# Second product of an MLP, in blocks of two row tiles by two column groups, every second block with seven products of block sums instead of eight

## The chip, the cores and the metric

One core of a Trainium2 chip runs the kernel. The metric is device time in microseconds (us) of the whole program, a median over runs. The profile comes from one execution, whose engines are PE (TensorE, matrix products; PEld is its loading of stationary operands), DVE (VectorE), ACT (ScalarE), POOL (GpSimd) and SP (SyncE, which issues the DMAs).

## The reference

One encoder layer on 256 tokens of width 2048: attention in two groups of heads, cross-attention to 256 memory tokens, then the part that is changed, with `x` of 256 x 2048, `w_mlp_in` of 2048 x 8192 and `w_mlp_out` of 8192 x 2048:

```
def squared_relu_mlp(h, w_mlp_in, w_mlp_out):
    return jnp.square(jax.nn.relu(h @ w_mlp_in)) @ w_mlp_out

        ff = squared_relu_mlp(x, w_mlp_in[l], w_mlp_out[l])
        x = layer_norm(ALPHA * x + ff, ln3_g[l], ln3_b[l])
```

All data is float32.

## The kernel before

Precision. Each float32 operand is written as a high and a low part: `split` lets ACT round the source to the high part (line 79) and DVE subtract it from the source to give the low part (line 80). A product is three matmuls, high by high, high by low and low by high (`mm3`, lines 145 to 147). Weights come from HBM in units of 1 MB, 128 x 2048, into one of three `raw` buffers; half a unit at a time, 128 x 1024, is split into `w_hi` and `w_lo`, of which there are four buffers each (`wsp`). I call such a split piece a part. So ACT and DVE can be four parts ahead of PE, and a part's buffer comes free when PE has used it for the last time.

The MLP. The 8192 hidden columns are worked off in four chunks (`c`, 16 row tiles of 128 each). In a chunk the first product makes the 16 tiles of the hidden activation in four groups of four (`hidden_group`, its matmuls are lines 194 and 199); `hidden` squares each one and splits it into `ht` (128 hidden rows, then 256 tokens high and 256 low). Then the second product goes over four column groups of 512 (`n`); for each one, `proj_tokens` and `tokens_mm` go over the 16 row tiles `k` and the two blocks `b` of 128 tokens, with a piece of `ht` stationary and 512 weight columns moving. The two sums, one for each token block, stand in PSUM and are added to `res` by DVE (line 755 or 758) when all 16 tiles are in. PSUM has eight tiles of 128 x 512 in two sets of four, `acc` and `att`, and successive groups alternate between the sets, so a group never waits for the tiles of the one before it. In the last chunk the fourth column group is done token block by token block, from parts that were all split ahead (`last_weights`, buffers `w0` and `w1`), so that the layer norm of block 0 runs under the products of block 1.

The order of the instructions on each engine is set when the program is built, by a scheduler that plays a timeline of its own. An engine takes its instructions in that order, and each waits for its semaphores. GpSimd has no work in the MLP but two small powers at the end.

Of the kernel before, what the change touches and what calls it, by code (L numbers as in the profile page):

```python
# [11 lines left out]
F32 = mybir.dt.float32  # L12
F32R = mybir.dt.float32r
# [5 lines left out]
P = 128  # L19
# [19 lines left out]
def encoder_kernel(ctx: ExitStack, tc: tile.TileContext, t, out):  # L39
# [6 lines left out]
    midp = ctx.enter_context(tc.tile_pool(name="midp", bufs=1))  # L46
    resp = ctx.enter_context(tc.tile_pool(name="resp", bufs=2))
    tmp = ctx.enter_context(tc.tile_pool(name="tmp", bufs=7))
    ptp = ctx.enter_context(tc.tile_pool(name="ptp", bufs=2))
    small = ctx.enter_context(tc.tile_pool(name="small", bufs=6))  # L50
    psA = ctx.enter_context(tc.tile_pool(name="psA", bufs=4, space=bass.MemoryType.PSUM))
    psT = ctx.enter_context(tc.tile_pool(name="psT", bufs=4, space=bass.MemoryType.PSUM))

# [23 lines left out]
    def split(hi, lo, src, scale=None, pinned=False):  # L77
        if scale is None:
            pin(nc.scalar.activation(hi, src, AF.Copy), pinned)  # L79
            return pin(nc.vector.tensor_tensor(out=lo, in0=src, in1=f(hi), op=ALU.subtract), pinned)  # L80
# [413 lines left out]
    def stats_tile():  # L494
        return [small.tile([P, 5, 6], F32, tag="bn", name="bn"), 0]
# [204 lines left out]
            w_mi0.append(s_mi0.next())  # L700


    s_in, s_mo = Stream(t["w_mi"][4:]), Stream(t["w_mo"])
    sts = [stats_tile() for _ in range(NB)]

    def hidden(ps, ht, j):
        tt = tmp_tile()
        lo, h = tt[:, 0:S], tt[:, S:2 * S]
        nc.scalar.activation(lo, ps[:, S:2 * S], AF.Copy)
        nc.vector.tensor_tensor(out=h, in0=ps[:, 0:S], in1=lo, op=ALU.add)  # L710
        nc.vector.scalar_tensor_tensor(out=lo, in0=h, scalar=0.0, in1=h, op0=ALU.max, op1=ALU.mult)
        split(ht[:, j, 0:S], ht[:, j, S:2 * S], lo)

    def last_weights(k):

        hi, lo = wide_w[0][:, k * 512:(k + 2) * 512], wide_w[1][:, k * 512:(k + 2) * 512]
        u, h = divmod(k, 4)
        if h == 0:
            wide_w[2] = raw_tile()
            nc.sync.dma_start(wide_w[2], t["w_mo"][s_mo.ap.shape[0] - 4 + u])  # L720
        split(hi, lo, wide_w[2][:, h * 512:(h + 2) * 512])
        return hi, lo

    G = 4

    def hidden_group(nexts, tiles, ht, j0):
# [7 lines left out]
        for i in range(G):  # L734
            hidden(outs[i], ht, j0 + i)

    for c in range(NCH):
        ht = big3(f"ht{c}")
        for g in range(CH // G):
            first = c == 0 and g == 0  # L740
            hidden_group((lambda k: w_mi0[k // 2]) if first else (lambda k: s_in.next()),
                         att_tile if g % 2 else acc_tile, ht, g * G)
            if first:
                side.extend(residual("ln2"))
        for n in range(4):
            tiles = att_tile if n >= 2 else acc_tile
            if c == NCH - 1 and n == 3:
                wide_w = [big.tile([P, 8192], F32R, tag="big", name=f"w{i}") for i in range(2)] + [None]
                ps = proj_tokens(None, ht, CH, 512, by_block=True, wide=last_weights, tiles=tiles)
            else:  # L750
                ps = proj_tokens(s_mo, ht, CH, 512, by_block=False, tiles=tiles)
            for b, o, w, p_ in ps:
                r = res[b][:, n * 512 + o:n * 512 + o + w]
                if c == 0:
                    nc.vector.scalar_tensor_tensor(out=r, in0=r, scalar=ALPHA, in1=p_[:, :w],
                                                   op0=ALU.mult, op1=ALU.add)
                else:
                    nc.vector.tensor_tensor(out=r, in0=r, in1=p_[:, :w], op=ALU.add)
                if c == NCH - 1:
                    stats(sts[b], r)  # L760

    g3, b3 = raw_tile(), raw_tile()
# [44 lines left out]
def _layout(i):  # L807
    f32 = np.float32
    a = {}
    x = np.asarray(i["x"])[0]  # L810
    a["x"] = x
    a["xT"] = np.ascontiguousarray(x.T.reshape(4, 4, P, S).transpose(0, 2, 1, 3)).reshape(4, P, 4 * S)
    a["mem"] = np.asarray(i["mem"])[0]
    w = np.asarray(i["w_in"])[0]
    qa, ka, va, cq, ckv, kr = np.split(w, np.cumsum([1024, 256, 256, 512, 512]), axis=1)
    a["w_qa"] = _rows(_pairs(qa, DH), 4, 512)
    a["w_ka"] = _rows(_pairs(ka, DH), 8, 256)
    a["w_vkr"] = _rows(np.concatenate([va, _pairs(kr, ROPE)], axis=1), 4, 320)
# [34 lines left out]
    a["w_mo"] = np.concatenate([_rows(mo[c * CH * P:(c + 1) * CH * P], 4, 512) for c in range(NCH)])  # L853
# [42 lines left out]
```

## Time and profile before

| what | us |
|---|---|
| median of three runs (lowest, highest) | 1122.93 (1122.74, 1123.06) |
| the profiled execution, time | 1123.25 |
| the same, span of the trace | 1121.4 |
| PE busy in the span | 1105.5 |
| DVE, ACT, POOL busy in the span | 729.0, 537.0, 38.2 |
| first product, chunk 0 (402.29 to 492.80 of the span) | 90.51 |
| first product, chunks 1 and 2 | 89.76 each |
| second product, chunks 0, 1 and 2 | 87.04 each |
| second product, chunk 3 | 87.85 |

The MLP is 710 us of the span. A stage's length here is the time from its first matmul to the first one of the next stage, on PE. The trace's time for one instruction includes a start and an end that overlap its neighbours', so what an instruction costs in a row of many is read from the distance of their starts.

### The profile page before, as it was taken

To read this page: it belongs to the slowest core of one execution; us is meant where nothing else is said; L and a number is where in the kernel's file an instruction comes from. 1 tells how busy PE (TensorE), PEld (TensorE's weight loads), DVE (VectorE), ACT (ScalarE), POOL (GpSimd) and SP (SyncE) were. 2 spreads that over 40 slices of the span, in tenths; PEclk is the share of its full clock that TensorE was granted. 3 is DMA by queue.
4 is the path that set the end of the run, shared out by engine and by line. 5 is a ranking of instruction groups with operands and counts; after the bars stand their busy time and mean duration, and the time that the engine had idled before them with its cause. 6 is when DMAs were issued, how large, how long until landed. Compare 5 with 4: busy or idle time off the path is not lost.

```text
span 1121.4 us, 15079 instructions
## 1 busy us (share of the span) xinstructions
PE 1105.5 (99%) x6004; PEld 954.2 (85%) x6004; DVE 729.0 (65%) x1036; ACT 537.0 (48%) x778; POOL 38.2 (3%) x45
## 2 busy tenths in 40 slices
PE   9999999999999989999999999999999999999996
PEld 6988899888998878888888888888888888888885
DVE  5878677687788677854545565555556454665575
ACT  6555565546576344543344454334444333544440
POOL 1402000000100000000000000000000000000000
PEclk9999999999999999999999999999999999999999
DMA  9664454476467426655555555555555555555562
GB/s 336 224 225 151 150 188 150 151 240 239 162 224 262 150 75 225 204 205 193 188 189 189 188 186 192 195 198 177 208 188 188 193 188 188 188 188 188 191 259 76
DMA packets 37942, 215.85 MB, mean 192 GB/s; under 512 B 4336, under 2 KB 5232, under 8 KB 14192
## 3 DMA queue, kind: packets, MB, share of 16 engines
q1 hardware_dynamic: 37872, 214.89, 54.6%
q8 instruction: 47, 0.77, 0.3%
q14 instruction: 23, 0.19, 0.1%
HBM read 212.78 MB, written 2.10 MB: 192 GB/s over the span
## 4 chain that ended last, share of the span: by engine, by line
PE 96%; DMA 2%; DVE 1%; ACT 0%; issue 0%; SPq 0%; POOL 0%; DVEq 0%; ACTq 0%
PE acc L146 12%; PE acc L145 12%; PE acc L147 12%; PE acc L194 11%; PE att L194 11%; PE att L147 6%; PE att L145 6%; PE att L146 6%; PE acc L199 5%; PE att L199 5%; PE acc L187 2%; PE acc L185 2%; PE acc L186 2%; PE att L534 1%; PE att L349 1%; DMA raw<-in_w_ka 1%
## 5 line engine op out<-in xcount | busy, mean ns | idle before, releaser
L80 DVE TENSOR_TENSOR w_lo<-raw,w_hi 128x1024 fp32r<-128x1024 f32 (+2 forms) x374 | 444.6, 1193 | 327.4 <-ACT w_hi L79 326.3
L79 ACT ACTIVATE w_hi<-raw 128x1024 fp32r<-128x1024 f32 (+2 forms) x374 | 386.5, 1036 | 459.0 <-PE acc L147 171.0
L194 PE MATMUL att<-x2t,w_hi 128*128 128x512 f32 x512 | 139.6, 394 | 0.0
L194 PE MATMUL acc<-x2t,w_hi 128*128 128x512 f32 x480 | 130.9, 394 | 0.0
L145 PE MATMUL acc<-w_hi,ht 128*128 128x512 f32 x256 | 99.6, 389 | 0.0
L146 PE MATMUL acc<-w_lo,ht 128*128 128x512 f32 x256 | 99.6, 389 | 0.0
L147 PE MATMUL acc<-w_hi,ht 128*128 128x512 f32 x256 | 99.6, 389 | 0.0
L194 PEld LDWEIGHTS att<-x2t,w_hi 128*128 128x128 f32 x512 | 88.1, 189 | 12.3
L194 PEld LDWEIGHTS acc<-x2t,w_hi 128*128 128x128 f32 x480 | 82.5, 189 | 11.5
L146 PE MATMUL att<-w_lo,ht 128*128 128x512 f32 x224 | 87.1, 389 | 0.0
L147 PE MATMUL att<-w_hi,ht 128*128 128x512 f32 x224 | 87.1, 389 | 0.0
L145 PE MATMUL att<-w_hi,ht 128*128 128x512 f32 x224 | 87.0, 389 | 0.0
L199 PEld LDWEIGHTS att<-x2t,w_lo 128*128 128x128 f32 x512 | 77.5, 189 | 10.2
L199 PEld LDWEIGHTS acc<-x2t,w_lo 128*128 128x128 f32 x480 | 72.6, 189 | 9.5
L199 PE MATMUL att<-x2t,w_lo 128*128 128x256 f32 x512 | 80.2, 281 | 0.0
L199 PE MATMUL acc<-x2t,w_lo 128*128 128x256 f32 x480 | 75.1, 281 | 0.0
L146 PE MATMUL acc<-w_lo,xt 128*128 128x512 f32 (+2 forms) x192 | 69.5, 363 | 0.2 <-DVE w_lo L80 0.2
L147 PE MATMUL acc<-w_hi,xt 128*128 128x512 f32 (+2 forms) x192 | 69.1, 361 | 0.0
L145 PE MATMUL acc<-w_hi,xt 128*128 128x512 f32 (+2 forms) x192 | 66.1, 364 | 1.0 <-ACT w_hi L79 1.0
L147 PEld LDWEIGHTS acc<-w_hi,ht 128*128 128x128 f32 x256 | 48.0, 188 | 10.0
L145 PEld LDWEIGHTS acc<-w_hi,ht 128*128 128x128 f32 x256 | 48.0, 188 | 10.0
L146 PEld LDWEIGHTS acc<-w_lo,ht 128*128 128x128 f32 x256 | 48.0, 188 | 10.0
(221 smaller groups left out, 1738.1 us busy)
## 6 DMA issues: line engine op xcount, KB each, us to landing
raw<-in_w_mi SPq DMA_DIRECT2D x64, 1024.0 KB, 4.8
raw<-in_w_mo SPq DMA_DIRECT2D x64, 1024.0 KB, 4.8
raw<-in_w_out SPq DMA_DIRECT2D x16, 1024.0 KB, 4.9
raw<-in_w_b SPq DMA_DIRECT2D x5, 1024.0 KB, 4.8
raw<-in_w_qa SPq DMA_DIRECT2D x16, 256.0 KB, 5.4
raw<-in_w_qa SPq DMA_DIRECT2D x4, 1024.0 KB, 4.9
raw<-in_w_ckv SPq DMA_DIRECT2D x4, 1024.0 KB, 5.1
raw<-in_w_cq SPq DMA_DIRECT2D x4, 1024.0 KB, 4.8
```

Of the source, the lines that this page charges most:

```text
L79: pin(nc.scalar.activation(hi, src, AF.Copy), pinned)
L80: return pin(nc.vector.tensor_tensor(out=lo, in0=src, in1=f(hi), op=ALU.subtract), pinned)
L145: nc.tensor.matmul(ps, ah, bh, start=start, stop=False)
L146: nc.tensor.matmul(ps, ah, bl, start=False, stop=False)
L147: nc.tensor.matmul(ps, al, bh, start=False, stop=stop)
L185: nc.tensor.matmul(ps, hi, xt[:, k, 0:S], start=k == 0, stop=False)
L186: nc.tensor.matmul(ps, hi, xt[:, k, S:2 * S], start=False, stop=False)
L187: nc.tensor.matmul(ps, lo, xt[:, k, 0:S], start=False, stop=k == nk - 1)
L194: nc.tensor.matmul(ps, hi[:, i * P:(i + 1) * P], xt[:, k, :], start=k == 0, stop=k == nk - 1)
L199: nc.tensor.matmul(ps[:, 0:S], lo[:, i * P:(i + 1) * P], xt[:, k, 0:S], start=False, stop=False)
L349: nc.tensor.transpose(pp[:, st * S + b * P:st * S + b * P + P], ev[:, b, st * P:(st + 1) * P], ident)
L534: nc.tensor.transpose(ps[:, o:o + P], x(b, k // 4)[:, (k % 4 + j) * P:(k % 4 + j + 1) * P], ident)
```

## The change

The second product takes two row tiles (k, k+1) and two column groups (1024 columns) at a time; I call this a unit. A unit is a 2 x 2 block product: A is two token blocks by two row tiles, B is two row tiles by two column groups, which makes eight block products of three matmuls each. Units go in a chunk by `q` (which half of the 2048 columns) and `p` (which pair of row tiles, 0 to 7). An even `p` is done with its eight block products (24 matmuls) in two parts. An odd `p` is done with seven (21 matmuls), by a scheme of Strassen's kind with sums of blocks: the sums of A are made on DVE in `hidden` and kept in `sums_h`; the sums of B are made on GpSimd, four additions of 128 x 512 for each odd unit, in `load_unit`; and these sums are split as weights are. Such a unit has four parts, of 1024, 512, 1024 and 1024 columns; I call them S1 (two blocks of B), S2 (one block), S3 and S4 (the sums). An even unit's two parts are E1 and E2. The last half of the last chunk (`c` 3, `q` 1) stays as it was. That leaves seven halves with four odd units each, 28 in all.

For a half, `pair_product` holds all eight PSUM tiles: `x11` to `x22` in `acc`, and the products `p1`, `p5`, `p6`, `p7` in `att`. When its units are done, `p1` is copied by ACT, and twelve additions bring the eight tiles into `res`: eight read PSUM and run on DVE; the last four read only SBUF and run on DVE for `q` 0, on GpSimd for `q` 1. The next half, or the next chunk's first product, needs the same eight tiles.

Buffers: `ht` is one tile for all chunks, `wx` is a new one that holds two units' `raw2` and two units' `sums_w`, and the pools of the attention are closed to make room for `sums_h`. `w_mo` is laid out in the new order.

```
@@ hidden @@
-        split(ht[:, j, 0:S], ht[:, j, S:2 * S], lo)
+        return lo
+    def hidden(ps, j):
+        r = []
+        for i in range(2):
+            r.append(square(ps[i]))
+            split(ht[:, j + i, 0:S], ht[:, j + i, S:2 * S], r[i])
+        if strassen(j // 2):
+            (a11, a21), (a12, a22) = [(x[:, 0:P], x[:, P:S]) for x in r]
+            s = tmp_tile()
+            s1, s2, s3, s4 = [s[:, o:o + P] for o in range(0, 4 * P, P)]
+            for o, a, b, op in ((s1, a21, a22, ALU.subtract), (s3, a11, a21, ALU.subtract),
+                                (s2, s1, a11, ALU.subtract), (s4, a12, s2, ALU.add)):
+                nc.vector.tensor_tensor(out=o, in0=a, in1=b, op=op)
+            split(sums_h[:, j // 4, 0, :], sums_h[:, j // 4, 1, :], s)
+    def strassen(p):
+        return p % 2 == 1
@@ new functions @@
+    def load_unit(chunk):
+        if not units or units[0][0] != chunk:
+            return
+        c, q, p = units.pop(0)
+        seven = strassen(p)
+        raw = raw_tile() if seven else raw2[p // 2 % 2]
+        nc.sync.dma_start(raw, t["w_mo"][(c * 2 + q) * (CH // 2) + p])
+        s = None
+        if seven:
+            s = sums_w[p // 2 % 2]
+            b12, b22, b21 = [raw[:, o:o + 512] for o in (0, 1024, 1536)]
+            def add(out, a, b):
+                nc.gpsimd.tensor_tensor(out=out, in0=a, in1=b, op=ALU.add)
+            add(s[:, 0:512], raw[:, 512:1024], b12)
+            add(s[:, 1024:1536], s[:, 0:512], b22)
+            add(s[:, 512:1024], b22, b12)
+            add(s[:, 1536:2048], s[:, 1024:1536], b21)
+        loaded.append((raw, s))
+    def pair_product(c, q):
+        x11, x12, x21, x22 = [acc_tile() for _ in range(4)]
+        p1, p5, p6, p7 = [att_tile() for _ in range(4)]
+        n = CH // 2
+        for p in range(n):
+            load_unit(c)
+            raw, s = loaded.popleft()
+            k = 2 * p
...
+            if strassen(p):
+                first, last = p == 1, p == n - 1
+                for src, todo in ((raw[:, 512:1536], ((p1, a(k, 0), first), (x12, sm(3), False))),
+                                  (raw[:, 1536:2048], ((x11, a(k + 1, 0), False),)),
+                                  (s[:, 0:1024], ((p5, sm(0), first), (p7, sm(2), first))),
+                                  (s[:, 1024:2048], ((p6, sm(1), first), (x21, a(k + 1, 1), False)))):
+                    for (hi, lo), (ps, (ah, al), start) in zip(part(src), todo):
+                        mm3(ps, ah, al, hi, lo, start, last)
+            else:
+                for i in range(2):
+                    w = part(raw[:, i * 1024:(i + 1) * 1024])
+                    for (hi, lo), to in zip(w, ((x12, x22), (x11, x21))):
+                        for b in range(2):
+                            ah, al = a(k + i, b)
+                            mm3(to[b], ah, al, hi, lo, p == 0 and i == 0, to[b] is x22 and p == n - 2 and i == 1)
...
+        rest = nc.gpsimd if q == 1 else nc.vector
+        first_add(r22, x22)
+        m1 = tmp_tile()
+        nc.scalar.activation(m1, p1, AF.Copy)
+        first_add(r12, x12)
+        first_add(r11, x11)
+        add(r12, r12, p5)
+        add(r22, r22, p5)
...
+        add(u2, m1, p6)
+        add(u3, u2, p7)
+        first_add(r21, x21)
+        add(r11, r11, m1, eng=rest)
+        add(r12, r12, u2, ALU.subtract, rest)
+        add(r21, r21, u3, eng=rest)
+        add(r22, r22, u3, ALU.subtract, rest)
...
@@ the loop over chunks @@
+            if g == CH // G - 1:
+                load_unit(c)
+                load_unit(c)
...
+        for q in range(2):
+            if c < NCH - 1 or q == 0:
+                pair_product(c, q)
+                continue
```

GpSimd, which has nothing to do in the MLP before, gets 112 additions for the weights' sums, in the order of the units, and behind each chunk's last unit four for `res`.

PE within the second product of chunk 0, before: for one row tile, the two token blocks (`att_5430`, `att_5431`) in turn, three matmuls each.

```order
L147 MATMUL att_5431<-w_hi_5502,ht0_4233 128x512
L145 MATMUL att_5430<-w_hi_5502,ht0_4233 128x512
L146 MATMUL att_5430<-w_lo_5503,ht0_4233 128x512
L147 MATMUL att_5430<-w_hi_5502,ht0_4233 128x512
L145 MATMUL att_5431<-w_hi_5502,ht0_4233 128x512
L146 MATMUL att_5431<-w_lo_5503,ht0_4233 128x512
```

And now, within half `q` 0 of chunk 0: the end of an odd unit (part S4 is `w_hi_5278` and `w_lo_5279`) and the start of the even unit behind it (E1 is `w_hi_5289` and `w_lo_5290`).

```order
L146 MATMUL att_5058<-w_hi_5278,sums_h_4239 128x512
L146 MATMUL acc_5054<-w_hi_5278,ht_4238 128x512
L146 MATMUL acc_5053<-w_hi_5289,ht_4238 128x512
L147 MATMUL att_5058<-w_lo_5279,sums_h_4239 128x512
L148 MATMUL att_5058<-w_hi_5278,sums_h_4239 128x512
L147 MATMUL acc_5054<-w_lo_5279,ht_4238 128x512
L148 MATMUL acc_5054<-w_hi_5278,ht_4238 128x512
L146 MATMUL acc_5055<-w_hi_5289,ht_4238 128x512
L146 MATMUL acc_5052<-w_hi_5289,ht_4238 128x512
L146 MATMUL acc_5054<-w_hi_5289,ht_4238 128x512
L147 MATMUL acc_5053<-w_lo_5290,ht_4238 128x512
L148 MATMUL acc_5053<-w_hi_5289,ht_4238 128x512
```

The scheduler has put the products with high parts ahead of those that need the low ones. E1 stands in the buffers that S1 of the odd unit had; S1's last matmul is nine ahead of the first row here, so that E1's low part is first needed 19 matmuls after it.

DVE in chunk 1, before, where one column group ends and the next one is under way (the splits on both sides belong to the next groups):

```order
L80 TENSOR_TENSOR w_lo_6674<-raw_6671,w_hi_6673 128x1024
L758 TENSOR_TENSOR res0_1487<-res0_1487,acc_6495 128x512
L758 TENSOR_TENSOR res1_1488<-res1_1488,acc_6496 128x512
L80 TENSOR_TENSOR w_lo_6690<-raw_6671,w_hi_6689 128x1024
L80 TENSOR_TENSOR w_lo_6708<-raw_6705,w_hi_6707 128x1024
```

And now, where half `q` 0 of chunk 1 ends: from part S4 of its last unit (`w_lo_6823`) to S2 of the second unit of `q` 1 (`w_lo_6906`), with E1 and E2 of the first one (`w_lo_6858`, `w_lo_6874`) between; `acc_6522` is `x21`.

```order
L81 TENSOR_TENSOR w_lo_6823<-wx_4240,w_hi_6822 128x1024
L843 TENSOR_TENSOR res0_1487<-res0_1487,acc_6521 128x512
L843 TENSOR_TENSOR res0_1487<-res0_1487,acc_6520 128x512
L81 TENSOR_TENSOR w_lo_6858<-wx_4240,w_hi_6857 128x1024
L846 TENSOR_TENSOR res0_1487<-res0_1487,att_6525 128x512
L846 TENSOR_TENSOR res1_1488<-res1_1488,att_6525 128x512
L81 TENSOR_TENSOR w_lo_6874<-wx_4240,w_hi_6873 128x1024
L846 TENSOR_TENSOR res0_1487<-res0_1487,tmp_6833 128x512
L846 TENSOR_TENSOR tmp_6840<-tmp_6833,att_6526 128x512
L843 TENSOR_TENSOR res1_1488<-res1_1488,acc_6522 128x512
L81 TENSOR_TENSOR w_lo_6896<-raw_6789,w_hi_6895 128x1024
L81 TENSOR_TENSOR w_lo_6906<-raw_6789,w_hi_6905 128x512
```

Two additions between splits have become twelve, woven into the splits of the next half.

PE where the second product of chunk 0 ends and the first product of chunk 1 begins, before: the last matmul of the one, then the four tiles of the first group in turn.

```order
L147 MATMUL att_5431<-w_hi_5552,ht0_4233 128x512
L194 MATMUL acc_5571<-x2t_4110,w_hi_5577 128x512
L194 MATMUL acc_5572<-x2t_4110,w_hi_5577 128x512
L194 MATMUL acc_5573<-x2t_4110,w_hi_5577 128x512
L194 MATMUL acc_5574<-x2t_4110,w_hi_5577 128x512
L199 MATMUL acc_5571<-x2t_4110,w_lo_5578 128x256
```

And now (`acc_5382` is `x21`, and `acc_5704` takes its place in PSUM):

```order
L148 MATMUL acc_5382<-w_hi_5675,ht_4238 128x512
L195 MATMUL acc_5701<-x2t_4110,w_hi_5707 128x512
L195 MATMUL acc_5702<-x2t_4110,w_hi_5707 128x512
L195 MATMUL acc_5703<-x2t_4110,w_hi_5707 128x512
L200 MATMUL acc_5701<-x2t_4110,w_lo_5708 128x256
L200 MATMUL acc_5702<-x2t_4110,w_lo_5708 128x256
```

Further on in the same group, on PE, the fourth tile comes in for the first time:

```order
L195 MATMUL acc_5701<-x2t_4110,w_hi_5749 128x512
L195 MATMUL acc_5702<-x2t_4110,w_hi_5749 128x512
L195 MATMUL acc_5703<-x2t_4110,w_hi_5749 128x512
L195 MATMUL acc_5704<-x2t_4110,w_hi_5707 128x512
L200 MATMUL acc_5704<-x2t_4110,w_lo_5708 128x256
```

The fourth tile's first matmul has moved behind 15 matmuls of 512 columns and 12 of 256.

More of the change, by code (lines that the diff above doesn't have):

```diff
@@ L45, in encoder_kernel @@
     wsp = ctx.enter_context(tc.tile_pool(name="wsp", bufs=4))
[L46 removed]
     resp = ctx.enter_context(tc.tile_pool(name="resp", bufs=2))
     tmp = ctx.enter_context(tc.tile_pool(name="tmp", bufs=7))
[L49 removed]
     small = ctx.enter_context(tc.tile_pool(name="small", bufs=6))
+    early = ExitStack()
+    midp = early.enter_context(tc.tile_pool(name="midp", bufs=1))
+    ptp = early.enter_context(tc.tile_pool(name="ptp", bufs=2))
     psA = ctx.enter_context(tc.tile_pool(name="psA", bufs=4, space=bass.MemoryType.PSUM))
@@ L700, in encoder_kernel, with square @@
             w_mi0.append(s_mi0.next())
-    s_in, s_mo = Stream(t["w_mi"][4:]), Stream(t["w_mo"])
+    early.close()
+    late = ctx.enter_context(tc.tile_pool(name="late", bufs=1))
+    s_in = Stream(t["w_mi"][4:])
     sts = [stats_tile() for _ in range(NB)]
-    def hidden(ps, ht, j):
+    ht = big3("ht")
+    sums_h = late.tile([P, 4096], F32R, name="sums_h").rearrange("p (u l c) -> p u l c", l=2, c=512)
+    wx = big.tile([P, 8192], F32, tag="big", name="wx")
+    raw2, sums_w = [[wx[:, o:o + 2048] for o in (i, i + 2048)] for i in (0, 4096)]
+    def square(ps):
         tt = tmp_tile()
@@ L724, in encoder_kernel, with hidden_group @@
     G = 4
-    def hidden_group(nexts, tiles, ht, j0):
+    def hidden_group(nexts, tiles, j0):
         outs = [tiles() for _ in range(G)]
@@ L733, in hidden_group @@
                           x2t, k + i, KT)
-        for i in range(G):
-            hidden(outs[i], ht, j0 + i)
+        for i in range(0, G, 2):
+            hidden(outs[i:i + 2], j0 + i)
+    units = [(c, q, p) for c in range(NCH) for q in range(2) for p in range(CH // 2)
+             if not (c == NCH - 1 and q == 1)]
+    loaded = deque()
+    def load_unit(chunk):
[16 more added lines that the diff above has]
+        loaded.append((raw, s))
@@ L737, in encoder_kernel @@
     for c in range(NCH):
-        ht = big3(f"ht{c}")
         for g in range(CH // G):
             first = c == 0 and g == 0
+            if g == CH // G - 1:
+                load_unit(c)
+                load_unit(c)
             hidden_group((lambda k: w_mi0[k // 2]) if first else (lambda k: s_in.next()),
-                         att_tile if g % 2 else acc_tile, ht, g * G)
+                         att_tile if g % 2 else acc_tile, g * G)
             if first:
                 side.extend(residual("ln2"))
[L745 to L756, printed above, removed]
-                else:
@@ new lines, in encoder_kernel @@
+        for q in range(2):
+            if c < NCH - 1 or q == 0:
+                pair_product(c, q)
+                continue
+            s_ml = Stream(t["w_ml"])
+            for n in (2, 3):
+                if n == 3:
+                    wide_w = [big.tile([P, 8192], F32R, tag="big", name=f"w{i}") for i in range(2)] + [None]
+                    ps = proj_tokens(None, ht, CH, 512, by_block=True, wide=last_weights, tiles=att_tile)
+                else:
+                    ps = proj_tokens(s_ml, ht, CH, 512, by_block=False, tiles=acc_tile)
+                for b, o, w, p_ in ps:
+                    r = res[b][:, n * 512 + o:n * 512 + o + w]
@@ L852, in _layout @@
     mo = np.asarray(i["w_mlp_out"])[0]
-    a["w_mo"] = np.concatenate([_rows(mo[c * CH * P:(c + 1) * CH * P], 4, 512) for c in range(NCH)])
+    m = mo.reshape(NCH, CH // 2, 2, P, 2, 2, 512)
+    order = [m[:, :, i, :, :, j, :] for i, j in ((0, 1), (0, 0), (1, 1), (1, 0))]
+    m = np.stack(order, axis=4).transpose(0, 3, 1, 2, 4, 5).reshape(NCH * CH, P, 2048)
+    a["w_mo"] = m[:-CH // 2]
+    a["w_ml"] = _rows(mo[-CH * P:, 1024:], 4, 512)
     for n in ("ln1", "ln2", "ln3", "mem_ln"):
```

29 lines of the change are left out of this document (27 added, 2 removed).

## Prediction

> **What bounds the kernel now.** I read the page's shares first, then the chain that ended last, then the stages of the second product, then PE and DVE row by row.
>
> ```profile
> PE 1105.5 (99%) x6004; PEld 954.2 (85%) x6004; DVE 729.0 (65%) x1036; ACT 537.0 (48%) x778; POOL 38.2 (3%) x45
> PE 96%; DMA 2%; DVE 1%; ACT 0%; issue 0%; SPq 0%; POOL 0%; DVEq 0%; ACTq 0%
> 492.80:579.84 87.04, 87.04 (x385) 72.07 (x384) 46.85 (x51) 35.91 (x39) 0.00 (x0) 1.00 0.55 190
> 669.60:756.64 87.04, 87.04 (x385) 72.07 (x384) 46.85 (x51) 35.91 (x39) 0.00 (x0) 1.00 0.55 190
> 579.84:669.60 89.76, 89.76 (x514) 78.50 (x512) 52.05 (x71) 41.77 (x58) 0.00 (x0) 1.00 0.54 191
> ```
>
> The first line is busy time by engine, the second the engines' shares of the chain. The others are stages: window, length, busy time of PE, PEld, DVE, ACT and POOL, granted clock, DMA share, GB/s; two second products and, last, a first one. PE is busy for the whole of each at a granted clock of 1.00, DVE for 54% and POOL not at all. A second product is 384 matmuls of 512 columns, so one costs 87.04 / 384 = 0.2267 us. A matmul that disappears is worth that, as long as PE then waits for nothing.
>
> ```profile
> 1050.17 0.39 PE L147 MATMUL acc<-w_hi,ht 128*128 128x512 f32 x1
> 1050.60 1.06 ACT L79 ACTIVATE w_hi<-raw 128x1024 fp32r<-128x1024 f32 x1 [1.66 <-PE acc L147]
> 1051.69 1.23 DVE L80 TENSOR_TENSOR w_lo<-raw,w_hi 128x1024 fp32r<-128x1024 f32 x1 [1.50 <-ACT w_hi L79]
> 1054.41 1.23 DVE L80 TENSOR_TENSOR w_lo<-raw,w_hi 128x1024 fp32r<-128x1024 f32 x1 [1.49 <-ACT w_hi L79]
> L80 DVE TENSOR_TENSOR w_lo<-raw,w_hi 128x1024 fp32r<-128x1024 f32 x32 | 39.2, 1226 | 40.2 <-ACT w_hi L79 40.2
> ```
>
> This is the loop that feeds PE. The last matmul on a part starts at 1050.17, ACT takes the freed buffer at 1050.60, and DVE ends the new part at 1052.92, 2.75 us after. Then DVE idles for 1.49 us. The last line has one second product's 32 splits: 39.2 us of work, 40.2 us of waiting. The room the change can use is there.
>
> **What is removed.** 28 units lose three matmuls each: 84 x 0.2267 = 19.04 us on PE, all of it on the chain. Two units (one even, one odd) took 48 x 0.2267 = 10.88 us and would take 45, 10.20 us.
>
> **What is added for DVE and POOL.**
>
> ```profile
> 1078.29 2.36 DVE L80 TENSOR_TENSOR w_lo<-raw,w_hi 128x1024 fp32r<-128x1024 f32 x2
> 19.62 1.30 DVE L80 TENSOR_TENSOR w_lo<-raw,w_hi 128x512 fp32r<-128x512 f32 x2
> 691.08 1.28 DVE L758 TENSOR_TENSOR res<-res,acc 128x512 f32<-128x512 f32 x2
> 32.51 1.30 POOL L297 TENSOR_TENSOR tmp<-tmp 128x512 f32<-128x512 f32 x1 [6.72 <-DVE tmp L295]
> ```
>
> In a row, two splits of 1024 take 2.36 us, one of which is 1.23: each further one costs 1.13. One of 512, and one addition of 512, cost 0.6. Two units needed four splits of 1024, 4.5 us; now they need five and one of 512, 5 x 1.13 + 0.61 = 6.26 us of 10.20. The same sum for ACT, with 1.06 for each part, is under 6 us. Twelve additions for a half are 12 x 0.6 = 7.2 us more on DVE (4.8 for `q` 1) where it was four, 2.4. POOL's addition of 128 x 512 takes 1.30 us by itself, so an odd unit's four are 5.2. Each engine alone has the time. The question is whether they have it together:
>
> ```profile
> 34.34 3.82 DVE L80 TENSOR_TENSOR w_lo<-raw,w_hi 128x1024 fp32r<-128x1024 f32 x4
> 34.37 4.96 POOL L297 TENSOR_TENSOR tmp<-tmp 128x512 f32<-128x512 f32 x1 [0.55 <-DVE rs_v L88]
> 90.76 1.21 DVE L80 TENSOR_TENSOR w_lo<-raw,w_hi 128x1024 fp32r<-128x1024 f32 x1
> 91.01 2.11 POOL L297 TENSOR_TENSOR tmp<-tmp 128x512 f32<-128x512 f32 x1 [1.15 <-DVE tmp L295]
> 91.89 1.78 DVE L298 TENSOR_TENSOR tmp<-tmp,rs_r 128x512 f32<-128x512 f32 x1
> 23.60 1.77 POOL L246 TENSOR_TENSOR tab_a<-tab_b 128x128 f32<-128x128 f32 x2
> 24.11 0.95 DVE L80 TENSOR_TENSOR w_lo<-raw,w_hi 128x512 fp32r<-128x512 f32 x1
> ```
>
> They don't. POOL's addition at 34.37 ran until 39.33: it stood while DVE did four splits (until 38.16) and then took 1.17 us. The one at 91.01 stood until DVE's split ended at 91.97, took 1.15 us, and DVE's next one, begun at 91.89, took 1.78 us, where an addition of that size takes 0.68: it ended 0.55 us behind POOL. Whenever both have two operands in SBUF, one stands. (At 32.51 DVE was reading PSUM, and POOL took its plain 1.30.) So their times add up: two units need 6.26 + 4 x 1.17 = 10.94 us of this common resource. That is over PE's new 10.20 by 0.74, and 0.06 more than the 10.88 of before: where this paces the work, seven products gain nothing.
>
> The Trainium skill, SBUF — State Buffer, Who interferes with whom, says that a DVE instruction with two SBUF inputs contends with a GpSimd instruction that reads SBUF, and that whichever issues first holds the pair for its whole instruction. On the exclusion the rows agree; on the turn they don't always, since by that rule the addition of 34.37 would have come in after one split and it came in after four. By the rule POOL's additions take their turn between splits and the sum is 10.94 for two units (the first rival); by the row at 34.37 DVE keeps its turn and the sum stays nearer to 10.20.
>
> **Which of it reaches PE.** Each chunk's first two odd units of `q` 0 are loaded and summed while the last group of the first product runs, where DVE is busy for 52.05 of 89.76 us. That leaves six odd units in each of three chunks and two in the last, 20. Bounds: 0 (POOL finds room in DVE's gaps of 1.49) and 20 x 0.74 = 14.8 us. In between, the slack decides. In the new order on PE, 45 matmuls for two units, E1's low part is first needed 19 matmuls (4.3 us) after the last one on the buffer it takes, and S4's 17 (3.9 us); with 2.75 us to make them, 1.55 and 1.15 us are left. One addition of 1.17 in the way is just covered, a second one is not. The other four parts have 2.7 us or more. DVE's free 3.9 us in 10.20 hold three additions; the fourth has to push a split. I take 0.3 for each of 20 units: 6 us.
>
> Sums too late are the other end of this: `sums_w` holds two units, so POOL may begin one 20.4 us before it is needed and may fall behind by 15 over a chunk. At 0.74 a unit, and 4.8 us of PSUM additions at the hand-over that POOL can run beside, it doesn't get there: 0.
>
> **The hand-overs.** A half holds all eight PSUM tiles, where groups alternated before. Seven hand-overs: three from `q` 0 to `q` 1, three to the next first product, one to the old code in chunk 3. `x21` ends with PE's last matmul; DVE still has E2's split, an addition and `u2` ahead of its addition. Counted from PE's last matmul: S4's buffer came free 21 matmuls ahead (-4.8), so its split ends at -2.0; in the order shown, with 0.6 for an addition and 1.13 for a split, two additions end at -0.8, E1's split at +0.3, two additions at +1.5, E2's split at +2.7, and `x21`'s addition at +4.5 for `q` 0 (three more) and +3.9 for `q` 1 (two). PE first needs the tile again after 21 matmuls (4.76) in the one case and after 15 of 512 and 12 of 256 (4.76) in the other. So without POOL it is covered by 0.3 to 0.9 us; with one addition of POOL in the way of a split it is late by up to 0.9. Bounds 0 and 7 x 1.17 = 8.2. POOL has sums to make at the three inner hand-overs and its four additions for `res` at the three outer ones; at the last it has nothing. I take 0.7 and 0.4: 3 x 1.1 = 3.3 us.
>
> **At no cost.**
>
> ```profile
> raw<-in_w_mo SPq DMA_DIRECT2D x64, 1024.0 KB, 4.8
> 1066.74:1088.50 21.76, 21.76 (x98) 18.02 (x97) 15.11 (x15) 12.19 (x13) 0.00 (x0) 1.00 0.69 261
> 1088.50:1099.40 10.90, 10.90 (x50) 9.03 (x49) 4.75 (x6) 0.98 (x2) 0.00 (x0) 1.00 0.28 98
> ```
>
> The first is the loads of these weights, with the time to landing, the others the third column group of chunk 3 and block 0 of the fourth. Sums of A: 16 additions of 128 x 128 and four splits of 512 in a chunk, under 8 us, in a stage where DVE idles for 37.7. The loads: as many MB, issued two units ahead; a load waits for POOL only where POOL still reads its buffer, and the next ones on SP's queue wait behind it, but 1 MB lands in 4.8 us, and raw units for the next first product are due later than the sums. The last half: the third column group now has DVE with twelve additions and four statistics, 9.6 us, on top of the 15.11 it has there. Together 24.7 of 21.76, but the splits that spill over are due one by one, 1.36 us apart, in the next 10.90 us, where DVE has 4.75. If that cover fails, it costs the 3 us that are over.
>
> **The sum.** 1123.25 - 19.0 + 6.0 + 3.3 = 1113.5 for the profiled execution (span 1121.4 and 1.85 around it), which is 0.3 above the median; I predict 1113.3 against 1122.93.
>
> **Rivals.**
> First, the common resource paces the second product (slower). DVE's two-operand work in a chunk is 16 x 3.13 + 4 x 0.6 = 52.5, POOL's 24 additions 28.1, and DVE's 16 PSUM additions are 9.6, half of them beside POOL or none: 85.4 to 90.2 against 87.04. In chunk 3 it is 39.2 to 41.6, with PE's own 40.8 as the floor, against 43.5. In all -7.6 to +7.6, and where waits between additions bring them to POOL's plain 1.30, 3.1 us a chunk more: up to +17. It decides from 1.24 us an addition on, with half the PSUM work covered. For it speaks the row at 24.11 (0.95, where one of the two at 19.62 takes 0.69, with POOL's second one of 23.60 begun in between), against it 34.37. I put it at 1128. The rule quoted above points here.
> Second, everything hides, as DVE's 40.2 us of waiting would suggest: 1104 to 1106.
> Third, DVE keeps its turn as at 34.37 and POOL starves: one turn lost in four is 1.17 us a unit, 7 in a chunk, which the 15 cover; two lost in four are 14 and a little more at the hand-over, and S3 is late at the end of three chunks, by 2 to 4 us each in place of the 6 above: 1113 to 1119, about the forecast.
>
> **How the numbers follow.** Forecast 0.42, first rival 0.30, second 0.15, third 0.13. About 0.2%, 2.2 us, is what a measurement of this kernel can tell from no change. Of the first rival I count 0.22 as slower, 0.05 as the same and 0.03 as faster; of the third 0.03 as the same, 0.01 as slower; the rest is faster: 0.69, 0.08, 0.23. The forecast's own range is 1107 to 1119. The whole one leaves out the best half of the second rival and the upper third of the first: 1105.5 to 1130.
>
> **What would show it.** Right: second products of 83 to 85 us in place of 87.04, PE waiting there in pieces under 1 us, most of them for DVE's `w_lo`, and POOL's additions at 1.2 to 3 us by their row, since standing counts as busy. Splits whose mean goes from 1.23 to 1.4 or more show that DVE stands too. First rival: stages of 87 us or more and DVE plus POOL (less what stands) filling them. Third: ACT waiting for POOL at S3. A hand-over that I misread shows as one PE wait of over 1 us at `x21`'s tile, six times. Wrong altogether would be a POOL addition that holds DVE for much more than 1.17 us, or PE held by high parts (ACT), which the order on PE now calls for sooner.

## The result

The changed kernel takes 1132.59 us (median of four runs, 1129.82 to 1134.51), the kernel before 1122.99: a ratio of 1.0083, 95% interval 1.0061 to 1.0104. It is slower by 9.6 us. The profiled execution took 1132.68 us, its span is 1130.9.

First the page's busy times and the shares of the chain, of the changed kernel:

```profile
PE 1099.0 (97%) x5920; PEld 938.0 (83%) x5920; DVE 919.5 (81%) x1216; ACT 588.5 (52%) x857; POOL 285.1 (25%) x169
PE 86%; DVE 10%; issue 3%; ACT 1%; DMA 1%; SPq 0%; POOL 0%; DVEq 0%; ACTq 0%
```

84 matmuls are gone, as the change says (6004 to 5920). DVE, which held 1% of the chain, now holds 10%, and its busy time grew by 190 us. Next the stages (window, length, busy time of PE, PEld, DVE, ACT and POOL, granted clock, DMA share, GB/s): three second products, a first product, and the last second product with the end.

```profile
492.21:582.71 90.50, 84.62 (x361) 66.65 (x360) 85.31 (x78) 48.90 (x58) 57.49 (x27) 1.00 0.51 183
672.51:763.36 90.85, 85.98 (x362) 67.84 (x360) 84.74 (x78) 48.69 (x58) 47.34 (x25) 0.98 0.49 177
853.17:944.03 90.86, 86.00 (x361) 67.85 (x360) 84.70 (x78) 48.68 (x58) 47.30 (x25) 0.98 0.49 177
582.71:672.51 89.80, 89.80 (x514) 78.40 (x513) 67.47 (x92) 43.42 (x62) 21.93 (x12) 1.00 0.55 196
1033.83:1130.90 97.07, 85.99 (x421) 71.96 (x419) 80.83 (x104) 38.93 (x46) 18.16 (x10) 0.96 0.42 155
```

The whole change is in the second products: 3.46, 3.81 and 3.82 us more than 87.04, 11.1 in all. The last stage is 1.1 shorter than before (98.2, from 1023.20 to 1121.4), the start 0.6 earlier, the first products 0.04 longer each. In the second products DVE is busy for 93 to 94% of the time. The groups of the page say why its work has become so long (behind the bar busy time and mean ns, then idle time; L81 is the line of `split` that was L80):

```profile
L81 DVE TENSOR_TENSOR w_lo<-wx,w_hi 128x1024 fp32r<-128x1024 f32 x112 | 184.3, 1671 | 28.8 <-ACT w_hi L80 27.9
L789 POOL TENSOR_TENSOR wx<-raw 128x512 f32<-128x512 f32 x56 | 105.0, 1896 | 346.5 <-DMA raw<-in_w_mo 205.9
L789 POOL TENSOR_TENSOR wx<-wx,raw 128x512 f32<-128x512 f32 x56 | 118.9, 2124 | 8.3 <-DVE w_lo L81 6.1
```

A split took 1226 ns before, and one from `wx` takes 1671 here; an addition on POOL took 1.30 us by itself and takes 1.90 to 2.12. Both engines stand. The timelines of DVE and POOL in one piece of a second product show them side by side (start, time, how many instructions the row holds, and in brackets the idle time before and what ended it):

```profile
857.45 1.21 DVE L81 TENSOR_TENSOR w_lo<-wx,w_hi 128x1024 fp32r<-128x1024 f32 x1
859.99 4.22 DVE L81 TENSOR_TENSOR w_lo<-wx,w_hi 128x1024 fp32r<-128x1024 f32 x2 [0.26 <-ACT w_hi L80]
864.14 1.78 DVE L81 TENSOR_TENSOR sums_h<-tmp,sums_h 128x512 fp32r<-128x512 f32 x1
865.85 2.31 DVE L81 TENSOR_TENSOR w_lo<-wx,w_hi 128x1024 fp32r<-128x1024 f32 x1
869.82 1.21 DVE L81 TENSOR_TENSOR w_lo<-wx,w_hi 128x1024 fp32r<-128x1024 f32 x1
858.74 4.39 POOL L789 TENSOR_TENSOR wx<-raw 128x512 f32<-128x512 f32 x2 [7.82 <-DVE w_lo L81]
863.09 3.98 POOL L789 TENSOR_TENSOR wx<-wx,raw 128x512 f32<-128x512 f32 x2
871.11 3.53 POOL L789 TENSOR_TENSOR wx<-raw 128x512 f32<-128x512 f32 x2 [4.03 <-DVE w_lo L81]
```

Until 858.74 POOL is idle, and DVE's split takes 1.21 us. Then POOL makes one unit's four additions, until 867.07, and in that time DVE's splits take 2.11 us each on average, then 2.31, and one of 512 columns 1.78. From 868 POOL is idle again and a split is back at 1.21. POOL doesn't fall behind: it waits (7.82 and 4.03 us) until DVE has read the old sums and freed their buffer, and in the trace of the MLP neither ACT nor DVE has a wait that POOL ends.

On PE the time is lost in pieces of 0.4 to 1 us, and in one large one in each chunk, where half `q` 0 ends. PE there, in chunk 2:

```profile
908.44 0.40 PE L148 MATMUL att<-w_hi,sums_h 128*128 128x512 f32 x1
911.48 0.50 PE L147 MATMUL att<-w_lo,sums_h 128*128 128x512 f32 x1 [2.64 <-DVE w_lo L81]
911.82 0.54 PE L148 MATMUL att<-w_hi,sums_h 128*128 128x512 f32 x1
912.58 0.63 PE L148 MATMUL acc<-w_hi,ht 128*128 128x512 f32 x1
913.00 0.63 PE L146 MATMUL acc<-w_hi,ht 128*128 128x512 f32 x1
915.14 0.48 PE L148 MATMUL acc<-w_hi,ht 128*128 128x512 f32 x1
PE att L147 <- DVE w_lo L81: 2.6, 1, 2.6
PE acc L147 <- DVE w_lo L81: 1.3, 3, 0.7
PE acc L146 <- DVE res L843: 0.8, 1, 0.8
```

The last three rows are the whole chunk's waits of PE (total, how many, longest). The long one is for the low part of S4 in the first odd unit of `q` 1: its products go to one `att` and one `acc` tile, as at 911.48 and 912.15, where S3's go to `att` alone. DVE begins that split at 909.14. After the wait ten matmuls take 3.98 us in place of 2.27, most of them 0.43 apart, some 1.7 us more. The wait of 0.8 is for the addition that frees `x21`'s tile.

Added up by the distance of their starts, PE loses 8.9 us in this chunk: 2.0 ahead of the hand-over (until DVE's first addition to `res`, at 892.74), 7.0 from there to 915.5, and nothing in the 28.6 us that are left. Until 915.5 DVE is busy for 61.45 of 62.29 us, behind it for 23.25 of 28.57.

### The profile page after: what moved, and what is told of

The parts are those of the page before. It is cut to its first block, busy times and chain, and to the rows that moved or that the text cites. A ratio compares the mean times of both kernels' runs of the same rounds, so it can differ in the third digit from the quotient of the medians.

```text
span 1130.9 us, 15403 instructions
## 1 busy us (share of the span) xinstructions
PE 1099.0 (97%) x5920; PEld 938.0 (83%) x5920; DVE 919.5 (81%) x1216; ACT 588.5 (52%) x857; POOL 285.1 (25%) x169
## 4 chain that ended last, share of the span: by engine, by line
PE 86%; DVE 10%; issue 3%; ACT 1%; DMA 1%; SPq 0%; POOL 0%; DVEq 0%; ACTq 0%
PE acc L147 12%; PE acc L148 12%; PE acc L146 12%; PE acc L195 11%; PE att L195 11%; DVE w_lo L81 6%; PE acc L200 5%; PE att L200 5%; PE att L147 3%; PE att L148 2%; PE att L146 2%; PE acc L188 2%; PE acc L186 2%; PE acc L187 2%; DVE res L846 1%
## 5 line engine op out<-in xcount | busy, mean ns | idle before, releaser
L81 DVE TENSOR_TENSOR w_lo<-raw,w_hi 128x1024 fp32r<-128x1024 f32 (+2 forms) x318 | 391.6, 1244 | 123.3 <-ACT w_hi L80 122.1
L80 ACT ACTIVATE w_hi<-raw 128x1024 fp32r<-128x1024 f32 (+2 forms) x318 | 313.4, 992 | 293.7 <-PE acc L148 96.6
L81 DVE TENSOR_TENSOR w_lo<-wx,w_hi 128x1024 fp32r<-128x1024 f32 x112 | 184.3, 1671 | 28.8 <-ACT w_hi L80 27.9
L789 POOL TENSOR_TENSOR wx<-raw 128x512 f32<-128x512 f32 x56 | 105.0, 1896 | 346.5 <-DMA raw<-in_w_mo 205.9
L80 ACT ACTIVATE w_hi<-wx 128x1024 fp32r<-128x1024 f32 x112 | 115.8, 1057 | 126.4 <-PE acc L148 91.6
L147 PE MATMUL acc<-w_lo,ht 128*128 128x512 f32 x312 | 125.1, 401 | 3.8 <-DVE w_lo L81 3.8
L148 PE MATMUL acc<-w_hi,ht 128*128 128x512 f32 x312 | 122.9, 394 | 0.0
L789 POOL TENSOR_TENSOR wx<-wx,raw 128x512 f32<-128x512 f32 x56 | 118.9, 2124 | 8.3 <-DVE w_lo L81 6.1
L146 PE MATMUL acc<-w_hi,ht 128*128 128x512 f32 x312 | 99.5, 393 | 2.8 <-DVE res L843 1.6
L92 POOL TENSOR_TENSOR rs_r<-rs_v,mhalf 128x1 f32<-128x1 f32 (+2 forms) x18 | 17.3, 963 | 287.6 <-DVE rs_v L89 287.5
L146 PEld LDWEIGHTS acc<-w_hi,ht 128*128 128x128 f32 x312 | 58.6, 189 | 17.4 <-DVE res L843 2.4
L148 PEld LDWEIGHTS acc<-w_hi,ht 128*128 128x128 f32 x312 | 59.4, 190 | 12.1
```

Of the source, the lines that this page charges most:

```text
L92: nc.gpsimd.tensor_tensor(out=r[:, :n], in0=v[:, :n], in1=mhalf[:, :n], op=ALU.pow)
L146: nc.tensor.matmul(ps, ah, bh, start=start, stop=False)
L147: nc.tensor.matmul(ps, ah, bl, start=False, stop=False)
L148: nc.tensor.matmul(ps, al, bh, start=False, stop=stop)
L789: nc.gpsimd.tensor_tensor(out=out, in0=a, in1=b, op=ALU.add)
```

## Experiments

Three theories. Theory 1: DVE and POOL take turns at what both need for operands from SBUF, so that their times add up, and this paces the second product. Theory 2: the steady part fits, and the time is lost where halves meet, since DVE has twelve additions there at once. Theory 3: it is lost because a half holds all eight PSUM tiles and groups don't alternate between two sets any longer. Times below are medians; each ratio is against runs of the kernel before on the same chip.

**POOL's additions cut to 16 columns.** The sums of the weights are left out but for 16 of 512 columns each; the rest is a constant that two fills set ahead of the MLP. Number and order of the instructions stay.

```
+    for w in sums_w:
+        nc.gpsimd.memset(w, 0.01)
...
-            add(s[:, 0:512], raw[:, 512:1024], b12)
...
+            for i in range(4):
+                add(s[:, i * 512:i * 512 + 16], raw[:, 512:528], raw[:, i * 512:i * 512 + 16])
```

> Of each of GpSimd's additions for the weights' sums only 16 of 512 columns are done (the rest of the sums is a constant, so the result is not the reference's); everything else, the splits of the sums too, stays. Theory 1 (DVE's splits and GpSimd's additions stand for each other, and what is lost at the hand-over from q 0 to q 1 is lost because of that): the second products fall from 90.5 to 90.9 us to 82 to 84, no wait of PE over 1 us is left at the hand-over, the mean of the odd units' splits from wx falls from 1.67 us to 1.25, and the time is 1104 to 1110. Theory 2 (DVE's twelve additions at the hand-over are too many by themselves, GpSimd or not): the wait of 2.8 us at the hand-over stays, 86 to 88 us a stage, 1118 to 1124. Theory 3 (all eight PSUM tiles in one half, with nothing to alternate with): as theory 2, the wait being for an addition that reads PSUM.

Measured: 1110.7 us, ratio 0.9888 (0.9874 to 0.9903). The second product of chunk 2, and the splits from there through the next first product:

```profile
841.22:923.96 82.74, 82.28 (x361) 67.42 (x360) 63.93 (x78) 48.69 (x58) 16.25 (x25) 1.00 0.53 194
L81 DVE TENSOR_TENSOR w_lo<-wx,w_hi 128x1024 fp32r<-128x1024 f32 x33 | 40.1, 1230 | 23.6 <-ACT w_hi L80 23.1
```

With the same instructions, but POOL reading little, splits take 1230 ns again, DVE's busy time falls from 84.70 to 63.93 and the stage by 8.1 us, to 82.74. The hand-overs and the PSUM tiles are those of the changed kernel, so theories 2 and 3 can't carry the loss by themselves, and no wait of PE for a PSUM tile is left. The total is 0.7 us above theory 1's range: this stage has the length of the one in the run with fills below, but starts 3.6 us later (841.22 against 837.64), since the two fills ahead of the MLP delayed DVE's layer norm by 3.2 us (last section).

**The sums on DVE.** One word:

```
-                nc.gpsimd.tensor_tensor(out=out, in0=a, in1=b, op=ALU.add)
+                nc.vector.tensor_tensor(out=out, in0=a, in1=b, op=ALU.add)
```

> The weights' sums are made by DVE in place of GpSimd. Theory 1: the common resource has 6.26 + 4 x 0.6 = 8.7 us of work in two units where it had 10.9, so DVE is the busier (some 85% of 10.2) but stands for nobody: 84 to 87 us a second product, 1107 to 1118. Theory 2: DVE, already too full at the hand-over, gets 2.4 us more for two units: over 91 us a stage, 1133 to 1142.

Measured: 1110.69 us, ratio 0.9887 (0.9873 to 0.9902). The stage of chunk 2, and one of the two groups of sums from there through the next first product:

```profile
840.09:923.99 83.90, 82.93 (x362) 67.18 (x361) 77.58 (x102) 48.74 (x58) 0.68 (x1) 1.00 0.52 191
L789 DVE TENSOR_TENSOR wx<-raw 128x512 f32<-128x512 f32 x16 | 10.4, 684 | 0.3 <-DMA raw<-in_w_mo 0.2
```

DVE does 24 instructions more (102 to 78) and is busy for less time, 77.58 in place of 84.70. Moving work onto the busier engine makes the kernel faster by some 22 us. The stage comes out just below theory 1's 84 to 87.

**The last additions of `q` 0 later.** The four that read only SBUF are tied behind splits of the next half, so that the crowd at the hand-over is thinner.

```
+        if q == 0 and c < NCH - 1:
+            for t_ in ((r11, r11, m1), (r12, r12, u2, ALU.subtract), (r21, r21, u3), (r22, r22, u3, ALU.subtract)):
+                side.extend([lambda: None] * (6 if t_[0] is r11 else 1) + [lambda t_=t_: later(*t_)])
```

> The last four additions of q 0 (both operands in SBUF) no longer stand among the splits at the hand-over, but one each behind later splits of q 1. Theories 1 and 2 alike, if these four are what makes the hand-over late: PE's wait of 2.8 us there goes to under 1 us, and the slow clock behind it goes too: 3 x 3 to 5 us less, 1118 to 1124. If the hand-over is late by the lock as such, and not by these: 1128 to 1133, with the wait moved. Theory 3: no change, 1130 to 1134.

Measured: 1130.7 us, ratio 1.0068 (1.0053 to 1.0083). Chunk 2:

```profile
852.68:942.38 89.70, 85.47 (x361) 66.48 (x360) 84.80 (x78) 48.72 (x58) 48.90 (x25) 1.00 0.49 179
```

The wait of 2.6 us and the slow matmuls behind it are gone (granted clock 1.00 where it was 0.98). The stage is only 1.2 us shorter, and in chunk 0 only 0.1: PE now waits in other places, the longest 0.7 to 1.0 us, and until 925.7, further into `q` 1. So theories 1 and 2 as far as they laid it on these four additions missed, and 1128 to 1133, with the wait moved, came true.

**Every unit by eight products.** The new blocks, halves, buffers and PSUM use, without sums and with the old 24 matmuls for each unit. Without `p1` to `p7` a half has four additions to `res` in place of twelve, and holds only the four tiles of `acc`, which the next half takes again. The sums of the activations, other than the expectation says, are not made either.

```
     def strassen(p):
-        return p % 2 == 1
+        return False
```

> The same units, halves and buffers, but every unit by eight products, without sums of weights and without p1, p5, p6, p7 (the sums of the activations are still made and not used). Theories 1 and 2: PE paces it as before the change, 87 to 87.5 us a second product, 1121 to 1126. Theory 3 (the loss of the alternating PSUM tiles): x11 to x22 are handed over as in the changed kernel, and each of six hand-overs costs 1 to 3 us: 1128 to 1140.

Measured: 1123.62 us, ratio 1.0004 (0.9994 to 1.0014). Chunk 2:

```profile
846.16:933.21 87.05, 87.05 (x386) 72.07 (x384) 45.79 (x50) 35.69 (x39) 0.00 (x0) 1.00 0.54 191
```

PE is busy for all of 87.05 us. Taking the same four tiles again without alternating costs nothing here. All eight tiles are held in the run with 16 columns, which has no wait for one; together the two rule theory 3 out as the main cause.

**Eight products, and the sums besides.** The kernel just shown, with POOL's additions put back. Nothing reads them, so neither engine waits for the other's results or buffers; they only share.

```
-        if seven:
+        if p % 2:
             s = sums_w[p // 2 % 2]
```

> All units by eight products, in the new blocks and halves; GpSimd makes the 112 additions of the weights' sums as in the changed kernel, but nothing reads them, so that neither engine waits for the other's results. Theory 1 (DVE and GpSimd take turns, one instruction each; an addition costs the common time 1.2 to 1.3 us): two units need 4 x 1.13 for splits and 4 x 1.2 to 1.3 for additions, 9.3 to 9.7 of PE's 10.88 us, so it just fits: second products 87.0 to 89 us, the mean split up from 1.22 to 1.6 us or more, the mean addition about 2 us, total 1123 to 1130. Rival 1 (an addition holds DVE for all of its 2 us): 12.5 of 10.88, second products over 95 us, total over 1145. Rival 2 (the changed kernel lost its time to the chain of sums, splits and buffers, each waiting for the other, not to the sharing): the mean split stays at 1.23 us, second products 87.04, total 1123.

Measured: 1123.34 us, ratio 0.9998 (0.9989 to 1.0007). Chunk 2, and two of its groups:

```profile
846.80:933.85 87.05, 87.05 (x386) 72.10 (x385) 57.12 (x51) 35.73 (x39) 39.92 (x23) 1.00 0.53 191
L81 DVE TENSOR_TENSOR w_lo<-raw,w_hi 128x1024 fp32r<-128x1024 f32 x19 | 31.1, 1642 | 16.2 <-ACT w_hi L80 16.2
L788 POOL TENSOR_TENSOR wx<-wx,raw 128x512 f32<-128x512 f32 x12 | 23.2, 1930 | 0.5
```

Splits from `raw` take 1642 ns, those from `wx` 1390, so the sharing is there with no data between the engines, and rival 2's split of 1.23 is not what came. DVE's busy time rises by 11.3 us for 23 additions, 0.5 us each, and POOL stands for the rest: additions of 1.66 to 1.93 us, where I had expected 2, and splits of 1.41 over the MLP, where I had expected 1.6. PE loses nothing, since two units leave room (9.3 to 9.7 of 10.88 us). Here the sum stays below PE's time, and the sharing costs PE nothing.

**Fills in place of the additions.** The sums are left out; POOL writes constants of the same size, and reads nothing.

```
-            add(s[:, 0:512], raw[:, 512:1024], b12)
...
+            for i in range(4):
+                nc.gpsimd.memset(s[:, i * 512:(i + 1) * 512], 0.01)
```

> The changed kernel with the four additions of a unit replaced by four fills of 128 x 512 with a constant on GpSimd, which read nothing; the sums are left out, so the output is another. If only GpSimd's reading from SBUF is in DVE's way: splits 1.23 us, second products 82.7 to 83.2, total 1106 to 1108. If a fill holds DVE too (the first experiment had five of DVE's instructions of 0.55 us take 5.55 beside 3.54 us of fills): two units need 6.26 + 4 x 0.45 = 8.1 of 10.20 us, the mean split goes to 1.35 us or more, second products 83 to 85, total 1108 to 1114.

Measured: 1107.79 us, ratio 0.9863 (0.9848 to 0.9877). Chunk 2, and the splits from there through the next first product:

```profile
837.64:920.36 82.72, 82.25 (x362) 67.43 (x360) 63.62 (x78) 48.70 (x58) 16.55 (x33) 1.00 0.53 194
L81 DVE TENSOR_TENSOR w_lo<-wx,w_hi 128x1024 fp32r<-128x1024 f32 x32 | 38.6, 1222 | 22.3 <-ACT w_hi L80 21.7
```

Splits take 1222 ns: it is POOL's reading that stands in the way of these instructions of DVE, not its writing.

**Two sums on POOL, two on DVE.**

```
+            add(nc.gpsimd, s[:, 0:512], raw[:, 512:1024], b12)
+            add(nc.vector, s[:, 1024:1536], s[:, 0:512], b22)
+            add(nc.gpsimd, s[:, 512:1024], b22, b12)
+            add(nc.vector, s[:, 1536:2048], s[:, 1024:1536], b21)
```

> Of the four additions for a unit's sums two stay on GpSimd and two go to DVE. Theory 1 (common time, 0.6 us for an addition on DVE and 1.2 to 1.3 us for one on GpSimd): a chunk's 52.5 + 12 x 0.6 + 12 x 1.2 to 1.3 + 9.6 = 83.7 to 84.9 us, just over the floor: second products 84 to 86.5, total 1111 to 1120. Rival (what costs is each change of turn, and a chain of sums across two engines): second products 87 to 91, as long as with all four on GpSimd, total 1122 to 1134.

Measured: 1115.65 us, ratio 0.9932 (0.9917 to 0.9947).

```profile
842.19:927.24 85.05, 84.01 (x362) 66.84 (x361) 78.38 (x90) 48.87 (x58) 27.15 (x13) 1.00 0.51 190
```

This bears on the price. In the prediction's sum for a chunk, DVE's own part is 52.5 + 9.6 = 62.1 us. Here 85.05 - 62.1 - 12 x 0.6 = 15.75 is left for twelve additions, 1.31 us each. In the changed kernel 90.86 - 62.1 is left for 24, 1.20 each, and with the last additions later (89.70) 1.15. These are rough, since they count DVE's idle time as price (6.7 us here, 6.2 in the changed kernel). Two other readings need no such sum. Where splits and additions alternate without a gap, splits start 2.24 us apart (873.40, 875.64, 877.87 in the changed kernel) in place of 1.13: 1.11 us for an addition. And by DVE's busy time, against the 63.93 of the 16 columns, the 24 additions cost 84.70 - 63.93 = 20.8 us on POOL, 0.87 each, and 77.58 - 63.93 = 13.7 on DVE itself, 0.57 each; so part of POOL's time is covered. The rival, a cost for mixing the engines at all, is out: half the additions cost a good part less.

**The sums and the rest on DVE, the last additions later.** The second experiment with the third, and `rest = nc.vector` also for `q` 1.

> A version to keep: sums and the four additions for the result on DVE (GpSimd has nothing left in the second product), and in q 0 the last four additions later, behind splits of q 1. If what is left over the floor of 82.3 us in the version with the sums on DVE (83.9) is DVE's crowd at the hand-over, second products go to 82.7 to 83.4 and the total to 1108.5 to 1110. If it is spread over the units, nothing changes: 83.9, 1110.7.

Measured: 1108.92 us (1108.52 to 1109.13), ratio 0.9871 (0.9854 to 0.9887).

```profile
838.60:921.50 82.90, 82.60 (x361) 67.29 (x360) 77.66 (x102) 48.52 (x58) 0.00 (x0) 1.00 0.52 192
```

A stage is 1.0 us shorter than with the sums on DVE alone and 0.2 longer than with POOL's additions at 16 columns. This version leaves nothing out, and is faster than both kernels: by 14.4 us than the one before, by some 24 than the changed one.

## Why the prediction was wrong

What failed is the step "The hand-overs", and in "Which of it reaches PE" the choice that DVE keeps its turn. The forecast put 0.3 us for each of 20 odd units (6.0) and 3.3 for the hand-overs. Against the stage of 82.74 that the 16 columns leave, the three second products lost 7.8, 8.1 and 8.1 us, 24.0 in all, where 18 of the units and the hand-overs were to cost 5.4 + 3.3 = 8.7. By the distance of PE's starts, each chunk lost 2.0 us away from the inner hand-over, where six units at 0.3 make 1.8, and 6.4 to 7.0 around it, where 0.7 stood.

- *The hand-overs.* The prediction followed `x21`'s tile alone. There it was right: PE waits 0.8 us for it in each chunk, where 0.7 stood. What it left out is what the twelve additions do to the splits behind them, with POOL in the way. From 892.74 to 914.77 in chunk 2 DVE has no gap. By the prediction's prices its own work in these 22.0 us is 16.8 (eight splits of 1024, one of 512, twelve additions), and the other 5.2 it stands for POOL. S4, which the prediction had as the part with the least slack, 1.15 us, then comes 2.6 us late, behind two additions that took 2.38 us in place of 1.28, and takes 2.29 itself. Behind the wait are, in two chunks of three, 1.7 us of slow matmuls. The outer hand-overs, put at 0.4, show no wait at all.

```profile
905.69 1.21 DVE L81 TENSOR_TENSOR w_lo<-wx,w_hi 128x1024 fp32r<-128x1024 f32 x1
906.83 2.38 DVE L846 TENSOR_TENSOR res<-res,tmp 128x512 f32<-128x512 f32 x2
909.14 5.64 DVE L81 TENSOR_TENSOR w_lo<-wx,w_hi 128x1024 fp32r<-128x1024 f32 x3
906.98 3.36 POOL L789 TENSOR_TENSOR wx<-raw 128x512 f32<-128x512 f32 x2 [5.89 <-DVE w_lo L81]
```

- *The turn.* I chose between the rows at 34.37 (DVE did four splits while one addition stood) and 24.11 (DVE stood for POOL). In the MLP they take turns: splits of 2.11 and 2.31 beside additions of 2.0 to 2.2. The Trainium skill, SBUF — State Buffer, Who interferes with whom, gives the lock to whoever issues first; by that rule the row at 34.37 was the odd one. It stood alone, and why it came out so was not tried.
- *The price* held where the two alternate: 1.17 us of common time for an addition was forecast, 1.11 measured.
- *The slack* was counted unit by unit: "DVE's free 3.9 us in 10.20 hold three additions", the fourth was to push a split by 0.3. Away from the hand-over that came out in size, though with the turn misjudged this is in part luck: the 2.0 us fall on a few units, in waits of up to 1.0 us. But the additions of the hand-over need the same free time. At each inner one POOL's sums overlapped five of the eight PSUM additions; through the other three POOL waited for a buffer (5.89 us in all in chunk 2).
- *The first rival* named the cause and, with 1128 and up to +17, about the size; I had it at 0.30. That its sum for a chunk, 52.5 + 28.1 + 9.6 = 90.2, is so near the stages of 90.50 to 90.86 is partly luck. The two engines fill only the first 62 us of 91. Behind it DVE idles for 5.3 us and PE loses nothing.
- *The removal* held: 84 matmuls less. Without sharing the total falls by 15.5 us of 19.04 (fills), so even there 3.5 us don't come through, and the second rival's 1104 to 1106 was too low by 2 to 4.
- *At no cost* held: the sums of A and the loads leave the first products at 89.80 to 89.81.
- *POOL starves* (third rival): no. POOL waits for DVE's reading of old sums, and no wait of ACT or DVE in the MLP is for POOL.

What is shown: that POOL's reading from SBUF is the cause (16 columns, fills), and that splits lengthen without any data between the engines (eight products and the sums). That the loss falls at the hand-over is read from the trace. How much the crowd of twelve additions adds by itself, with the sums still on POOL, is open: the one run on it moved only four of them, and PE's waits moved along.

## What to carry to other kernels

Before giving two-operand work in SBUF to GpSimd to relieve DVE, add up both engines' times as if they were one engine, at DVE's price for DVE's work and about 1.1 us here for an addition of 128 x 512 on GpSimd, and compare with PE's time. Do it for the whole stage, and again for its densest stretch, as long as the buffers can't bridge it; here that was the 22 us at the hand-over. The same addition on DVE costs 0.6, so the idle engine is the dearer one. In the one run where the sum stayed below PE's time throughout, GpSimd's work was free (eight products and the sums: 1123.34 against 1123.33). Where two rows of a trace disagree on how a resource is granted, the one that stands under steady load is to be looked for, or both cases carried with even chances.

## What the runs showed of the hardware

A fill on POOL doesn't touch DVE's splits, which have two operands in SBUF (1222 ns, above), but it did hold instructions of DVE with a single one. In the first experiment the two fills of 128 x 2048 stood beside the layer norm ahead of the MLP. Below are POOL and DVE of that run, then DVE of the run with the sums on DVE, which has no fills:

```profile
396.60 3.54 POOL L722 MEMSET wx<- 128x2048 f32 x2
396.69 6.47 DVE L522 TENSOR_SCALAR res<-res,mv,rs_r 128x512 f32<-128x512 f32 x7 [0.66 <-POOL rs_r L92]
396.58 3.29 DVE L522 TENSOR_SCALAR res<-res,mv,rs_r 128x512 f32<-128x512 f32 x7 [0.66 <-POOL rs_r L92]
```

Seven instructions took 6.47 us in place of 3.29, 3.2 us more beside 3.54 us of fills. Taken one by one, only the first stood: 3.74 us, through both fills, though the second fill began 1.65 us after it. As in the row at 34.37, the turn was not handed over; no run tested why. The Trainium skill, SBUF — State Buffer, Who interferes with whom, says that a two-input instruction contends only with a GpSimd instruction that reads, while one-input forms that run in a two-port mode contend with any. The first half agrees with the 1222 ns. The second would explain the 6.47 us if these instructions ran in such a mode, which no run here shows.

And a wait of PE can cost more than its length: after the 2.6 us at 908.44 most of ten matmuls started 0.43 us apart, with a mean granted clock of 0.57 from 911.4 to 915.4 (0.98 over the stage). Chunk 0 has a wait as long without it (its row shows 1.00). The Trainium skill, TensorE: Matmul & The Clock Gate, Part 1: The HAM clock gate, halves the clock after an idle window of about 3.4 us, with windows that run freely. The spacing of 0.43 agrees with the half clock; a wait of 2.6 us, shorter than that window, was enough here in two chunks of three. No run tested why.
